# Loading and storing the last tile of a row normalisation as two DMAs of every second partition

## Chip, cores, metric

One core of a Trainium2 chip. The metric is device time in microseconds (us). All runs named below were fast (one core, granted clock 1.0). The span of a profile, from its first to its last instruction, is 1.6 to 2.1 us shorter than the time of the same run, so spans are compared with spans and times with times.

## The reference

```python
x = np.random.randn(32, 512, 1024).astype(np.float32)
sums = np.sum(np.abs(x), axis=-1, keepdims=True)
return (x / (sums + 1e-8)).astype(np.float32)
```

Each of 16384 rows of 1024 floats is divided by the sum of its absolute values. 67 MB come in and 67 MB go out.

## The kernel before

A tile is 128 partitions x 12 rows; the last one has 8 rows. Four tile buffers rotate. VectorE (DVE) sums the rows and multiplies most of them, ScalarE (ACT) multiplies the rest. Loads are issued from SyncE (SP), stores from ACT.

```python
R, BUFS, HEAD = 12, 4, 32
rows = [R] * ((per_partition - HEAD) // R + 2) + [HEAD - 2 * R]   # ten of 12, one of 8
def piece(flat, i):                  # the rows of DRAM that tile i takes
    head = flat[: P * HEAD, :].rearrange("(p r) d -> p r d", p=P)
    ...                              # cut: tiles 0 and 1, and the tiles of the body
    if i == len(rows) - 1:
        return head[:, 2 * R :, :]   # last tile: 8 rows of 4 KB, together 32 KB, per partition
...                                  # cut: pools, and normalize()
for i, k in enumerate(rows):
    x_tile = sbuf.tile([P, R, d], FP32)
    nc.sync.dma_start(out=x_tile[:, :k, :], in_=piece(x_flat, i))
    ...                              # cut: normalize(x_tile, ...)
    nc.scalar.dma_start(out=piece(out_flat, i), in_=x_tile[:, :k, :])
```

Of the kernel before, what the change touches and what calls it, by code (L numbers as in the profile page):

```python
# [1 line left out]

# [4 lines left out]

FP32 = mybir.dt.float32
EPS = 1e-8


@with_exitstack
def kernel(
    ctx: ExitStack,
    tc: tile.TileContext,
    x: bass.AP,
    out: bass.AP,
):
    nc = tc.nc
    P = nc.NUM_PARTITIONS  # L20

    x_flat = x.flatten_outer_dims()
    out_flat = out.flatten_outer_dims()
    n, d = x_flat.shape




    R = 12
    BUFS = 4  # L30
    HEAD = 32
    per_partition = n // P
    assert n % P == 0 and (per_partition - HEAD) % R == 0
    rows = [R] * ((per_partition - HEAD) // R + 2) + [HEAD - 2 * R]

    def piece(flat, i):
        head = flat[: P * HEAD, :].rearrange("(p r) d -> p r d", p=P)
        if i < 2:
            return head[:, R * i : R * (i + 1), :]
        if i == len(rows) - 1:  # L40
            return head[:, 2 * R :, :]
        a = P * (HEAD + R * (i - 2))
        return flat[a : a + P * R, :].rearrange("(p r) d -> p r d", p=P)

    sbuf = ctx.enter_context(tc.tile_pool(name="sbuf", bufs=BUFS))
    stats = ctx.enter_context(tc.tile_pool(name="stats", bufs=4))

    def normalize(x_tile, r0, k, kv):

        s = stats.tile([P, R], FP32)  # L50
        nc.vector.tensor_reduce(  # L51
            out=s[:, :k],
            in_=x_tile[:, r0 : r0 + k, :],
            axis=mybir.AxisListType.X,
            op=mybir.AluOpType.add,
            apply_absolute_value=True,
        )
        nc.vector.tensor_scalar_add(out=s[:, :k], in0=s[:, :k], scalar1=EPS)  # L58
        inv = stats.tile([P, R], FP32)
        nc.vector.reciprocal(out=inv[:, :k], in_=s[:, :k])  # L60
        nc.vector.tensor_mul(  # L61
            out=x_tile[:, r0 : r0 + kv, :],
            in0=x_tile[:, r0 : r0 + kv, :],
            in1=inv[:, :kv].unsqueeze(2).to_broadcast([P, kv, d]),
        )
        for r in range(kv, k):
            row = x_tile[:, r0 + r, :]
            nc.scalar.activation(  # L68
                out=row,
                in_=row,  # L70
                func=mybir.ActivationFunctionType.Copy,
                scale=inv[:, r : r + 1],
            )

    with tc.manual_schedule():
        for i, k in enumerate(rows):
            x_tile = sbuf.tile([P, R, d], FP32)
            nc.sync.dma_start(out=x_tile[:, :k, :], in_=piece(x_flat, i))  # L78


            if i == 0:
                normalize(x_tile, 0, k, k - 5)
            else:
                normalize(x_tile, 0, k, k - 1 if i + BUFS < len(rows) else k)
            nc.scalar.dma_start(out=piece(out_flat, i), in_=x_tile[:, :k, :])  # L85


# [1 line left out]
_INS = ['x']  # L89
_OUTS = [((32, 512, 1024), 'float32')]  # L90


# [23 lines left out]
```

## Time and profile before

| | before |
|---|---|
| time, median of the first 3 runs | 317.25 us (317.13 to 317.62) |
| span of the profiled run | 317.3 us (that run's time: 318.93 us) |
| the 16 DMA engines, share of the span | 98.5% |
| VectorE busy | 85% |
| last load: issued, landed, wanted | 247.6, 283.0, 285.3 us |
| last store: issued, landed | 303.2, 316.2 us |

Read it from the end: what has the last store waiting, and do the DMA engines have room before it? The prediction shows the views. The profiler's record of every DMA packet has its queue, start, duration and size. A data packet is the whole row block of one partition: 48 KB in 1.815 us for a 12-row tile, 32 KB in 1.213 us for the last one (medians). Besides these each DMA has 16 completion packets of 4 bytes, of 9 ns each.

### The profile page before, as it was taken

The page shows a single profiled execution, that of the slowest core. Times are in us where ns is not written, and L with a number is a line of the kernel's source. Part 1 is how long each engine was busy: PE and PEld are TensorE (multiplying, and loading weights), DVE is VectorE, ACT ScalarE, POOL GpSimd, SP SyncE. Part 2 cuts the span into 40 slices and gives each one's busy share as a digit, 9 for nine tenths or more (in the row PEclk, how much of TensorE's full clock was granted, in tenths as well). Part 3 has the DMA queues.
Part 4 walks back from the last instruction along what each step waited for, and adds up shares of the span by engine and source line. Part 5 has one row for each costly group of instructions (what it writes and reads, how often), then busy time and mean ns, then how long its engine had stood idle before and what let it go on. Part 6 is the DMA issues. An engine that isn't in the chain of part 4 may idle for free.

```text
span 317.3 us, 170 instructions
## 1 busy us (share of the span) xinstructions
DVE 268.7 (85%) x44; ACT 13.5 (4%) x12; POOL 0.2 (0%) x4
## 2 busy tenths in 40 slices
DVE  0079999999999999989995996799699969999920
ACT  0010601001000000100100010000000000000000
POOL 0000000000000000000000000000000000000000
DMA  8999999999999999999999999999999999999994
GB/s 328 465 397 471 421 378 415 415 465 409 459 434 397 477 415 415 465 409 459 428 403 477 409 428 452 409 471 415 403 477 415 428 430 452 397 477 415 403 425 215
DMA packets 3168, 134.22 MB, mean 423 GB/s; under 512 B 352, under 2 KB 352, under 8 KB 352
## 3 DMA queue, kind: packets, MB, share of 16 engines
q1 hardware_dynamic: 1584, 67.11, 49.6%
q10 hardware_dynamic: 1584, 67.11, 48.9%
HBM read 67.11 MB, written 67.11 MB: 423 GB/s over the span
## 4 chain that ended last, share of the span: by engine, by line
DVE 52%; DMA 34%; another core or an unknown queue 9%; issue 0%; SPq 0%; DVEq 0%; ACTq 0%
DVE s L51 27%; DVE x_tile L61 24%; DMA x_tile<-in_x_dram 18%; DMA out_dram<-x_tile 16%; DVE inv L60 1%; DVE s L58 0%; SPq L78 0%; DVEq L60 0%; ACTq L85 0%
## 5 line engine op out<-in xcount | busy, mean ns | idle before, releaser
L51 DVE TENSOR_REDUCE s<-x_tile 128x12 f32<-128x12288 f32 (+1 forms) x11 | 138.2, 12561 | 32.9 <-DMA x_tile<-in_x_dram 32.9
L61 DVE TENSOR_TENSOR x_tile<-x_tile,inv 128x11264 f32<-128x11264 f32 (+3 forms) x11 | 126.5, 11504 | 0.4
L68 ACT ACTIVATE x_tile<-x_tile,inv 128x1024 f32<-128x1024 f32 x11 | 12.2, 1142 | 153.6 <-DVE inv L60 153.6
L60 DVE RECIPROCAL inv<-s 128x12 f32<-128x12 f32 (+1 forms) x11 | 2.5, 226 | 0.9
L58 DVE TENSOR_SCALAR s<-s 128x12 f32<-128x12 f32 (+1 forms) x11 | 1.9, 173 | 0.4
L68 ACT ACT_TABLE_LOAD x1 | 1.3, 1283 | 17.8 <-DMA x_tile<-in_x_dram 17.8
L100 POOL MEMSET const-bfloat16-1.0<- 128x1 bf16 x1 | 0.1, 102 | 0.0
L100 POOL MEMSET const-uint8-127<- 128x1 uint8 x1 | 0.1, 102 | 0.0
L100 POOL MEMSET const-float32-0.0<- 128x1 f32 x1 | 0.1, 99 | 0.2 <-issue 0.2
L100 POOL MEMSET const-float32-1.0<- 128x1 f32 x1 | 0.1, 99 | 0.0
## 6 DMA issues: line engine op xcount, KB each, us to landing
x_tile<-in_x_dram SPq DMA_DIRECT2D x10, 6144.0 KB, 39.2
out_dram<-x_tile ACTq DMA_DIRECT2D x10, 6144.0 KB, 43.7
x_tile<-in_x_dram SPq DMA_DIRECT2D x1, 4096.0 KB, 35.4
out_dram<-x_tile ACTq DMA_DIRECT2D x1, 4096.0 KB, 13.0
```

The source lines that it names most:

```text
L51: nc.vector.tensor_reduce(out=s[:, :k], in_=x_tile[:, r0 : r0 + k, :], axis=mybir.AxisListType.X, op=mybir.AluOpType.add, apply_absolute_v ...
L58: nc.vector.tensor_scalar_add(out=s[:, :k], in0=s[:, :k], scalar1=EPS)
L60: nc.vector.reciprocal(out=inv[:, :k], in_=s[:, :k])
L61: nc.vector.tensor_mul(out=x_tile[:, r0 : r0 + kv, :], in0=x_tile[:, r0 : r0 + kv, :], in1=inv[:, :kv].unsqueeze(2).to_broadcast([P, kv, d]),)
L68: nc.scalar.activation(out=row, in_=row, func=mybir.ActivationFunctionType.Copy, scale=inv[:, r : r + 1],)
L100: nc = _bacc.Bacc("TRN2", target_bir_lowering=False, num_devices=1)
```

## The change

No reason came with it. The likely intent is to have the halves of the last transfer move independently while each half still has partitions from the whole range, 0 to 127, of the on-chip memory (SBUF).

```diff
-            nc.sync.dma_start(out=x_tile[:, :k, :], in_=piece(x_flat, i))
+            parts = 2 if i == len(rows) - 1 else 1
+            for j in range(parts):
+                nc.sync.dma_start(
+                    out=x_tile[j::parts, :k, :], in_=piece(x_flat, i)[j::parts, :, :]
+                )
 ...
-            nc.scalar.dma_start(out=piece(out_flat, i), in_=x_tile[:, :k, :])
+            for j in range(parts):
+                nc.scalar.dma_start(
+                    out=piece(out_flat, i)[j::parts, :, :], in_=x_tile[j::parts, :k, :]
+                )
```

## The prediction

> **What bounds the kernel now.** I read the page first, then the waits of the engines and of the load queue, the stage table, the timeline of the last 60 us, and last the single packet records of the DMA. The page:
>
> ```profile
> DVE 268.7 (85%) x44; ACT 13.5 (4%) x12; POOL 0.2 (0%) x4
> DMA packets 3168, 134.22 MB, mean 423 GB/s; under 512 B 352, under 2 KB 352, under 8 KB 352
> q1 hardware_dynamic: 1584, 67.11, 49.6%
> q10 hardware_dynamic: 1584, 67.11, 48.9%
> L51 DVE TENSOR_REDUCE s<-x_tile 128x12 f32<-128x12288 f32 (+1 forms) x11 | 138.2, 12561 | 32.9 <-DMA x_tile<-in_x_dram 32.9
> ```
>
> VectorE (DVE) is busy 85% and its only waits, 32.9 us, are for loads. Loads (q1) and stores (q10) together fill 49.6 + 48.9 = 98.5% of the time of all 16 DMA engines. So the transfers bound the kernel. The 3168 packets are 22 DMAs x 16 completion packets (352, the small ones) and 22 x 128 data packets: one per partition.
>
> The stage table (core 0: us, length, busy DVE, ACT, POOL, clock, DMA share, GB/s) shows where DMA time is lost:
>
> ```profile
> 60.00:100.00 40.00, 39.90 (x6) 1.15 (x1) 0.00 (x0) 1.00 1.01 436
> 220.00:260.00 40.00, 33.90 (x6) 0.00 (x0) 0.00 (x0) 1.00 1.00 432
> 260.00:290.00 30.00, 29.83 (x5) 0.00 (x0) 0.00 (x0) 1.00 0.99 429
> 290.00:304.00 14.00, 13.00 (x4) 0.00 (x0) 0.00 (x0) 1.00 0.92 400
> 304.00:310.00 6.00, 0.00 (x0) 0.00 (x0) 0.00 (x0) 1.00 1.01 434
> 310.00:317.30 7.30, 0.00 (x0) 0.00 (x0) 0.00 (x0) 1.00 0.52 224
> ```
>
> From 60 to 290 us there is no room; the end has a little. The timeline of that end, and the DMA issues with their time to landing:
>
> ```profile
> 272.38 12.96 DVE L61 TENSOR_TENSOR x_tile<-x_tile,inv 128x12288 f32<-128x12288 f32 x1
> 285.25 8.68 DVE L51 TENSOR_REDUCE s<-x_tile 128x8 f32<-128x8192 f32 x1
> 294.48 8.69 DVE L61 TENSOR_TENSOR x_tile<-x_tile,inv 128x8192 f32<-128x8192 f32 x1
> ```
> ```profile
> x_tile<-in_x_dram SPq DMA_DIRECT2D x1, 4096.0 KB, 35.4
> out_dram<-x_tile ACTq DMA_DIRECT2D x1, 4096.0 KB, 13.0
> ```
>
> The last load is issued at 247.6 and lands at 283.0, 35.4 us later. DVE takes it up at 285.3, when it leaves tile 9: it had 2.3 us to spare. The last store is issued at 303.2 and lands at 316.2.
>
> The packet records have queue, start, duration and size, not the engine; I chained them by ends. A 48 KB packet takes 1.815 us (27.1 GB/s, times 16 is 433), a 32 KB one 1.213. In the last load 13 of the 16 chains run in step within 0.5 us (first packets 255.55 to 256.03, ends 277.9 to 278.4), three are later (281.3, 281.7, 282.6). Tile 9's store ends at 303.3 to 303.8 on the 13 and at 306.19 on the last one, which does its eight 32 KB packets from there without a pause: 306.19 + 8 x 1.21 = 315.87, exactly where data ends; landing and end of program take 1.43 us more. So **one late DMA engine that never pauses sets the end**; the 13 others finish at 313.8 to 313.9 and have 2 us to spare.
>
> [...]
>
> [...]
>
> [...]
>
> [...]
>
> **The change part by part.** It removes nothing: 4 MB in and 4 MB out as before, 32 KB packets as before, and DVE still waits for both loads and the store still for the whole multiply.
>
> It adds two DMA issues. One on the load queue takes 0.33 us, at 248.0, 7.5 us before the first packet of this load can start (the one before still fills the queue): hidden. One on the store queue takes 0.34 us, while each engine has four packets (4.9 us) of the first half to do: hidden. 2 x 16 more completion packets at 9 ns, two per engine: 0.02 us. [...] Sum without anything else: 317.25 + 0.1 = 317.4.
>
> It may move one thing: which engine serves which partition. [...] 32 KB then take up to 2 x 1.213 = 2.43 us. With a pair offset of some 0.2 us (my estimate from the 0.5 us spread) it is 2.23, so +1.0 per packet.
>
> Load: eight packets x 1.0 = +8 us on the 13 chains: ends 286 to 286.5, landing 0.4 later at 286.4 to 286.9, against 285.3 wanted. DVE is 1 to 1.6 us late; the last store is issued at about 304.8. But the chains are also 8 us behind with tile 8's and 9's stores: 303.3..303.8 + 8 = 311.4..311.9. Store: 8 x 2.23 = 17.8, ends 329.3 to 329.7, plus 1.43: **331**. [...]
>
> **The rivals.**
> (a) [...] Then 317.4.
> (b) *Only the store suffers* (the loads' packets alternate with 1.8 us store packets, which could absorb it): the 13 chains start together at 304.05, 8 x 2.43 = 19.4, ends 323.5, plus 1.43: 324.9.
> (c) *Only the load suffers*: 311.4..311.9 + 8 x 1.21 + 1.43 = 322.5 to 323.
> (d) *A false dependency*: strided slices of a tile are taken as overlapping, and the second half is issued only when the first has landed. The load then has a hole that the queued stores fill, but may land 1 to 3 us later than 283.0; the two stores one after the other cost an issue and a landing, 0.8 + 0.4 us. Together 318 to 320.
> (e) *A gain*: smaller DMAs spread the late engines' work. Against it: the share of each engine is fixed, eight packets; at most the 2 us by which the late one trails, 0.6%.
>
> **Range and chances.** I give 0.40 to (a), 0.07 to (d) and (e) together, 0.05 to (c), 0.10 to (b), and 0.38 to both with full or half force (325 to 331). Slower by over 2% means over 323.6: all of (b), nearly all of the double case and little else, with some weight for a worse store: 0.51. Faster by 2% would need 6 us where at most 2 are to be had: 0.02. The rest is 0.47. The middle of two humps, at 317.4 and at 325 to 331, is 324; the range from 316.6 to 331.5 covers both.
>
> **What would show it.** Right if in the changed profile the 32 KB packets take over 2 us, the last store lands about 20 us or more after its issue instead of 13.0, the DMA share stays near 1 at the end while GB/s falls to about half, and the last reduce starts after 286. Wrong, and (a), if 32 KB packets still take 1.21 and the landing stays at 13.0 to 13.4. (d) would show as a wait of the load queue for its own first half. Lengthened packets in the load alone or the store alone decide (b) and (c). [...]

The sum "without anything else" came to 317.4: 317.25, the 0.02 us of the completion packets (9 ns each in the trace), and an allowance of under 0.1 us. I took it that pairs of engines, running in step, would hold each other up, so that a packet takes up to twice its 1.213 us. The factor of two, and with it 2.23 us, is my estimate; no view of the kernel before shows a packet lengthened so. The sums 331, 324.9 and 322.5 to 323 rest on it. Rival (a) is that no packet is held up.

The alternation that rival (b) names is in the packet records. From 80 to 240 us 1578 packets start in the kernel before; 1322 of them have just one packet that starts as they end (within 6 ns), and in all 1322 that one is of the other queue.

## The result, and the profile after

| | before | after |
|---|---|---|
| time, median of 6 runs | 316.97 us (316.56 to 317.62) | 317.40 us (317.15 to 318.76) |
| ratio of fast runs | | 1.0017 (95%: 0.9998 to 1.0036) |

A ratio is the mean time of one kernel's fast runs over that of the other's fast runs of the same rounds, so it is not quite the ratio of the medians quoted beside it. The change is neither faster nor slower. The forecast was 324, slower with a chance of 0.51.

From the page of the changed kernel, the DMA packets and queues, and the DMA issues (count, KB each, median us to landing):

```profile
DMA packets 3200, 134.22 MB, mean 423 GB/s; under 512 B 384, under 2 KB 384, under 8 KB 384
q1 hardware_dynamic: 1600, 67.11, 49.8%
q10 hardware_dynamic: 1600, 67.11, 48.9%
x_tile<-in_x_dram SPq DMA_DIRECT2D x2, 2048.0 KB, 28.8
out_dram<-x_tile ACTq DMA_DIRECT2D x2, 2048.0 KB, 12.0
```

There are 32 more packets, the completion packets of two more DMAs, 16 each, as foretold. Bytes are unchanged and the shares nearly so. The stage table of the changed kernel (us, length, busy DVE, ACT, POOL, clock, DMA share, GB/s; a packet counts in full where it starts, so a share can pass 1):

```profile
260.00:290.00 30.00, 29.51 (x5) 0.00 (x0) 0.00 (x0) 1.00 1.02 428
290.00:304.00 14.00, 10.91 (x4) 0.00 (x0) 0.00 (x0) 1.00 0.96 417
304.00:310.00 6.00, 0.00 (x0) 0.00 (x0) 0.00 (x0) 1.00 0.96 415
310.00:317.00 7.00, 0.00 (x0) 0.00 (x0) 0.00 (x0) 1.00 0.55 239
```

This is the decisive view. While only the split store runs (304 to 310) the engines still move 415 GB/s; had each packet taken the 2.23 us of the forecast, it would be about 235 (16 times 32 KB in 2.23 us). The packet records say the same: all 128 packets of the split store took 1.213 us, none longer; in the last load the median is 1.213, with 21 packets at 1.6 to 2.1.

The timeline of the changed kernel at the last tile:

```profile
247.60 1.17 SPq L81 DMA_DIRECT2D x_tile<-in_x_dram  x2
283.16 8.69 DVE L51 TENSOR_REDUCE s<-x_tile 128x8 f32<-128x8192 f32 x1 [0.32 <-DMA x_tile<-in_x_dram]
```

The two loads are issued back to back within 1.17 us, so no false dependency holds the second (rival d). The pair of issues took longer than twice the 0.33 us counted, but stayed hidden. New is a small wait, 0.32 us, of VectorE for the last load. The absolute times are not comparable with the kernel before to the microsecond: tile 9's load, which the change cannot touch, let VectorE start at 256.36 us in this profile and at 258.85 in the other. Which engines run late, and by how much, differs between the two profiles.

What is comparable is the distance between two loads. I take the median over the 16 engines of the completion packets of tile 9's load and of the last load: 253.9 to 278.1, so 24.2 us, before; 255.0 to 282.2, so 27.2 us, after. The last load came 3.0 us later behind the one ahead of it.

That leaves two questions. Why did the store packets not get longer: do packets never hold each other up, or does it depend on which partitions a DMA takes? And where do the 3.0 us come from?

### The profile page after: what moved, and what is told of

Its sections match the earlier page's. It is cut to its first block, busy times and chain, and to the rows that moved or that the text cites. A ratio compares the mean times of both kernels' runs of the same rounds, so it can differ in the third digit from the quotient of the medians.

```text
span 317.0 us, 174 instructions
## 1 busy us (share of the span) xinstructions
DVE 268.8 (85%) x44; ACT 13.5 (4%) x12; POOL 0.2 (0%) x4
## 4 chain that ended last, share of the span: by engine, by line
DVE 44%; DMA 32%; another core or an unknown queue 18%; SPq 0%; issue 0%; DVEq 0%; ACTq 0%
DVE s L51 23%; DVE x_tile L61 20%; DMA x_tile<-in_x_dram 16%; DMA out_dram<-x_tile 16%; DVE inv L60 0%; SPq L81 0%; DVE s L58 0%; DVEq L60 0%; DVEq L51 0%; ACTq L91 0%
## 5 line engine op out<-in xcount | busy, mean ns | idle before, releaser
L51 DVE TENSOR_REDUCE s<-x_tile 128x12 f32<-128x12288 f32 (+1 forms) x11 | 138.2, 12563 | 30.7 <-DMA x_tile<-in_x_dram 30.7
L68 ACT ACT_TABLE_LOAD x1 | 1.3, 1283 | 17.8 <-DMA x_tile<-in_x_dram 17.8
```

The source lines that it names most:

```text
L51: nc.vector.tensor_reduce(out=s[:, :k], in_=x_tile[:, r0 : r0 + k, :], axis=mybir.AxisListType.X, op=mybir.AluOpType.add, apply_absolute_v ...
L68: nc.scalar.activation(out=row, in_=row, func=mybir.ActivationFunctionType.Copy, scale=inv[:, r : r + 1],)
```

## The experiments

Eight kernels ran, e1 to e4 in one call and on one chip, e5 to e8 in a second; all gave correct results, none was refused. Each left one profile. The edits are against the changed kernel. The table has the mean duration of the last tile's 32 KB packets (1.213 is undisturbed) and the distance between the last two loads as defined above.

| kernel | median us | ratio to before (95%) | load packet | store packet | load distance |
|---|---|---|---|---|---|
| before (packets of its profiled run) | 317.25 | | 1.217 | 1.221 | 24.2 |
| the change | 317.40 | 1.0017 (0.9998 to 1.0036) | 1.317 | 1.213 | 27.2 |
| e1 halves of the partitions | 332.48 | 1.0492 (1.0471 to 1.0513) | 1.985 | 2.223 | 34.2 |
| e2 every tile by every second | 321.03 | 1.0125 (1.0102 to 1.0149) | 1.229 | 1.213 | 24.2 |
| e3 last tile by every fourth | 320.13 | 1.0104 (1.0081 to 1.0128) | 1.221 | 1.223 | 29.9 |
| e4 last load only | 317.98 | 1.0040 (1.0005 to 1.0075) | 1.291 | 1.213 | 26.7 |
| e5 halves in SBUF, every second in DRAM | 332.29 | 1.0476 (1.0441 to 1.0511) | 1.712 | 2.405 | 30.7 |
| e6 every second in SBUF, halves in DRAM | 317.27 | 1.0012 (0.9971 to 1.0053) | 1.224 | 1.213 | 26.1 |
| e7 last store only | 318.07 | 1.0033 (0.9994 to 1.0071) | 1.223 | 1.213 | 24.2 |
| e8 last store by every eighth | 325.74 | 1.0269 (1.0236 to 1.0302) | 1.218 | 2.221 | 24.2 |

The kernel before had medians of 316.77 us (e1 to e4) and 316.95 us (e5 to e8) beside them.

**e1: does any choice of partitions lengthen the packets?** The same two DMAs, but of partitions 0-63 and 64-127.

```diff
-out=x_tile[j::parts, :k, :], in_=piece(x_flat, i)[j::parts, :, :]
+out=x_tile[j * w : (j + 1) * w, :k, :], in_=piece(x_flat, i)[j * w : (j + 1) * w, :, :]   # w = 64
```
and the store likewise.

> Last tile split into partitions 0-63 and 64-127 instead of every second partition. Theory P [...]: [...] a 32 KB packet takes about 2.4 us instead of 1.21, the last store about 10 us longer, total 325 to 331. Theory N [...]: packets stay at 1.21 us, total 317 to 318.5.

Theory P is that a choice of partitions can double the time of a packet, theory N that none does. 332.48 us, 5% slower: theory P; its 325 to 331 was 1.5 us short. From this kernel's timeline and stage table:

```profile
290.21 8.69 DVE L51 TENSOR_REDUCE s<-x_tile 128x8 f32<-128x8192 f32 x1 [7.30 <-DMA x_tile<-in_x_dram]
260.00:290.00 30.00, 22.74 (x4) 0.00 (x0) 0.00 (x0) 1.00 0.99 335
310.00:318.00 8.00, 0.00 (x0) 0.00 (x0) 0.00 (x0) 1.00 1.09 274
```

Between 260 and 290 the engines are as busy as ever (0.99) and move 335 GB/s instead of 429; in the stretch in which the store begins they move 274: busy without moving, as each packet takes longer for the same bytes. VectorE waits 7.30 us for the last load. The packets of the store have a median of 2.55 us, about twice 1.213. From the first of them at 310.2 us to the end of the last at 329.4 the store's 4.19 MB take 19.2 us: 218 GB/s, half of 433. So the loss is real, in loads (packets of 1.985 us on average) and in stores (2.223). What inside the chip causes it no run shows.

**e2: did the changed kernel only escape by luck of timing?** Every tile is split, so that the first loads run with all engines in step and no store beside them.

```diff
-            parts = 2 if i == len(rows) - 1 else 1
+            parts = 2
```

> Every tile, not just the last, loaded and stored as two DMAs of every second partition. Theories P and N: 48 KB packets stay at 1.815 us also in the first 17 us, where 16 engines start together and nothing else runs; total 317 to 320. Theory D [...]: the first load takes over 25 us instead of 17, packets there 2.7 to 3.6 us, total above 330.

The waits of this kernel's engines:

```profile
DVE s L51 <- DMA x_tile<-in_x_dram: 30.8, 5, 18.2
```

The first load took up 18.2 us of waiting, not over 25. In the kernel before it took 17.8 us. The engines are in step: their completion packets of the first half fall within 0.5 us (10.04 to 10.52). Packets that start in the first 17 us take 1.92 us on average, against 1.90 in the kernel before, with a median of 1.815 in both. Theory D, that packets with step 2 do get longer while the engines are in step, falls. The time, 321.03, is 1 us above the expected range, a ratio of 1.0125. Of the loss of some 4 us, 0.3 us is a later first packet (2.03 us instead of 1.73), and in the profiled run the latest engine ends 3.3 us behind the median one (316.8 against 313.5), against 2.0 before (315.9 against 313.9). Most of the loss, and why that engine is later, I did not settle.

**e3: what do added DMAs cost the load?** Four DMAs of every fourth partition.

```diff
-            parts = 2 if i == len(rows) - 1 else 1
+            parts = 4 if i == len(rows) - 1 else 1
```

> Last tile as four DMAs of every fourth partition for load and store. Theory T (each added completion packet uses up a turn of the load queue, which a 1.8 us store packet then fills): the time from the landing of the load before to the landing of this one grows by about 1.8 us per added DMA, so some 5 us over the kernel before; VectorE starts the last reduce 2 to 4 us late and the last store is issued at 305 to 307; total 318 to 321. Theory N or P without turns: load lands at 283, total 317 to 318.

Theory T holds in each number but one: the first of the store's four issues came at 304.7 us, a little before the expected 305. The load distance is 29.9 us, 5.7 more than before, for three added DMAs (3 x 1.8 = 5.4). From this kernel's timeline and stage table:

```profile
286.72 8.69 DVE L51 TENSOR_REDUCE s<-x_tile 128x8 f32<-128x8192 f32 x1 [3.27 <-DMA x_tile<-in_x_dram]
304.00:310.00 6.00, 0.64 (x1) 0.00 (x0) 0.00 (x0) 1.00 0.82 345
```

VectorE starts the last reduce 3.27 us late, and this time it shows: the last store comes so late that the DMA engines stand idle for it (0.82 between 304 and 310). 320.13 us, 1% slower, with store packets at 1.22: 32 partitions with step 4 do not lengthen them either.

**e4 and e7: which half of the change delays the load?** Only the load split (e4), only the store split (e7).

```diff
 # e4
+            parts = 1
             for j in range(parts):
                 nc.scalar.dma_start(
```
```diff
 # e7
-            parts = 2 if i == len(rows) - 1 else 1
+            parts = 1            # for the load
+            parts = 2 if i == len(rows) - 1 else 1   # again ahead of the store
```

> Only the load of the last tile is split by every second partition, the store is one DMA as before. Theory T: the last load lands 2 to 3 us later after the load before it than in the kernel before, as in the changed kernel; total the same as the changed kernel within 0.5 us, as the store adds nothing. If the later landing was only that run's chance, it is gone here.

> Only the store of the last tile is split by every second partition. Theory T (turns): no change of the last load, which lands 24 to 25 us after the load before it as in the kernel before; store packets 1.21, last store landing within 13.5 us of its first issue; total within 0.5 us of the kernel before.

The load distance is 26.7 us in e4 and 24.2 us in e7: the delay belongs to the load's own second DMA and not to chance. Both totals are the same as before at the 2% limit; e4's interval lies just above 1 (1.0005), e7's contains it. In median e4 is 0.6 us above the changed kernel, and e7 1.1 us above the kernel before, a little over what I expected; the mean ratio, 1.0033, does not separate it from 1. One expectation failed: e7's last store landed 14.2 us after its first issue (300.9 to 315.1), not within 13.5, although every packet took about 1.213.

**e5 and e6: SBUF or DRAM?** In e1 both sides, on-chip memory (SBUF) and DRAM, were halved, so a conflict by DRAM address could also have done it. e5 takes halves in SBUF and every second row block in DRAM, e6 the reverse.

```diff
 # e5
-out=x_tile[j::parts, :k, :], in_=piece(x_flat, i)[j::parts, :, :]
+out=x_tile[j * w : (j + 1) * w, :k, :], in_=piece(x_flat, i)[j::parts, :, :]
 # e6
+out=x_tile[j::parts, :k, :], in_=piece(x_flat, i)[j * w : (j + 1) * w, :, :]
```
and the stores likewise.

> The last tile's two DMAs take SBUF partitions 0-63 and 64-127, but in DRAM every second row block. Theory S (the loss of the first run with halves is on the SBUF side, by partition): 32 KB packets of 2.0 us in the load and 2.5 in the store, total 330 to 334 as there. Theory H (it is on the HBM side, by address: 64 neighbouring row blocks): packets 1.21, total 317 to 319.

> The reverse: every second SBUF partition, but in DRAM the first and the second 64 row blocks. Theory S: packets 1.21 in the store, total 317 to 319. Theory H: packets 2.0 to 2.5, total 330 to 334.

e5 332.29 us, e6 317.27. The last DMA issue line of the page, e5 first:

```profile
out_dram<-x_tile ACTq DMA_DIRECT2D x2, 2048.0 KB, 16.5
```
and e6:
```profile
out_dram<-x_tile ACTq DMA_DIRECT2D x2, 2048.0 KB, 11.3
```

Theory S: which SBUF partitions go together decides (store packets of 2.405 us in e5), the DRAM addresses don't (1.213 in e6). The load packets of e5 averaged 1.71 us, not the expected 2.0; no run shows why.

**e8: is it the step that protects?** The store alone, in eight DMAs of every eighth partition.

```diff
-            parts = 2 if i == len(rows) - 1 else 1      # ahead of the store; the load has parts = 1
+            parts = 8 if i == len(rows) - 1 else 1
```

> Only the store of the last tile is split, into eight DMAs of every eighth partition, 16 partitions [...] in each. [...] Theory S [...]: packets about 2.2 to 2.4 us, last store about 9 us longer, total 324 to 328. Theory R (a step between partitions is what protects[...]): packets 1.21, total 317 to 319.

Theory S is that the choice of partitions counts, and not the step alone. 325.74 us with store packets of 2.22. The stage table of e8:

```profile
290.00:304.00 14.00, 10.37 (x4) 0.00 (x0) 0.00 (x0) 1.00 1.01 427
304.00:310.00 6.00, 0.00 (x0) 0.00 (x0) 0.00 (x0) 1.00 1.10 240
```

As soon as the split store runs, 427 GB/s become 240 with the engines still full. Theory R falls: a step of eight is as bad as neighbouring halves (store packets of 2.22 us in e8 and in e1). By the partitions that one DMA takes, with the mean of the store packets: all 128 (1.221), 64 with step 2 (1.213) and 32 with step 4 (1.223) keep the full rate, 64 neighbours (2.223) and 16 with step 8 (2.221) do not. What sets these apart no run shows.

## Why the prediction was wrong, and where it was right

**What held.** The DMA engines bound the kernel: e3, where an idle spell of these engines lengthens the run, agrees. That one late engine sets the end no run tested; the changed kernel's profile shows one again, ending at 315.45 us against a median of 314.08. The sum "without anything else", 317.4, is what was measured, but to the digit only by luck: it leaves out the later load, and it takes the span of the profiled run (317.3) for the median time (317.25), while that run's own time was 318.93. The two added issues were hidden, no semaphore and no dependency wait appeared, and no gain came (rivals d and e).

**The step that failed** is the estimate of 2.23 us for a 32 KB packet. All 128 store packets took 1.213 us, and in e2 engines in step were no slower than before (1.92 us against 1.90). The ground of the estimate, an assumption about which engine serves which partitions, was not shown: the records name neither engine nor partition. The outcome was that of rival (a), which I gave 0.40. That no choice of partitions lengthens the packets is refuted by e1; that every second partition does not is what was measured. In the kernel before no 32 KB packet took longer than 1.46 us, so no view spoke for doubled packets, and (a) deserved the larger share. The forecast of 324 was the middle between two outcomes and the sum of neither.

**The doubling itself was right where packets do get longer**, and for the store so were its sizes. e1 is the kernel that I had in effect predicted: I had 2.23 us per store packet, it has 2.22; data ending at 329.3 to 329.7, it ends at 329.4; 331 in all, and its span is 330.9. Rival (b), the store alone at half rate, was worked out as 324.9; e8's span is 324.5. Some of this is luck: 2.22 is the mean of a mix, with a median of 2.55 and 25 of the 128 packets under 1.6 us. The load was mis-sized: its packets took 1.99 us instead of 2.23, and yet it landed at 290.1 us instead of 286.4 to 286.9, because of the turn described next and because the store packets beside it grew from 1.815 to 1.98 us on average.

**What I had missed** is the turn. I counted the added completion packets as 9 ns each. In the load, one costs more: e3, e4, e6 and the changed kernel put the last load 5.7, 2.5, 1.9 and 3.0 us further behind, and e7 and e8, whose loads are whole, put it 0.0 us. The packets of the two queues take turns, and a completion packet uses up a turn of the load queue: a store packet, mostly one of 1.815 us, goes before the next load packet. The packet records show it. Between 80 and 240 us all 1322 packets with just one follower are followed by the other queue in the kernel before (counted beside the prediction), and all 1248 in the changed kernel. From 60 us to the last landing, 87 load completion packets before and 124 after have just one follower: each time it is of the store queue, a 48 KB packet in 87 and 118 of the cases. Between the two medians that define the load distance, 128 store packets of 48 KB start in the kernel before, e2, e7 and e8, 144 in the changed kernel and e4, 143 in e6 and 176 in e3: about 16 more for each added load DMA, as many as it has completion packets. In e6, where hardly any load packet was slow, one turn is nearly all of it (1.9). In the changed kernel and e4 some slow load packets of up to 2.3 us, just where the second half begins, add 0.8 and 0.6 us per engine; why these occur in some runs only stays open. In e2, where the stores are split too, the distance is 24.2 again and the count 128; that the stores' own added completion packets give the turns back would explain it, but no run tests that. The later load hardly showed in the total, because what the load loses the stores gain, and the last load had 2.3 us to spare (VectorE waited 0.32 us); three turns exceed that, and e3 pays.

## What to carry to other kernels

Before you split a DMA by partitions, measure the packets of the very choice of partitions that you mean, in load and store: here the store of every second (packets of 1.213 us) or fourth partition (1.22) kept the full rate, neighbouring halves (2.22) or every eighth (2.22) ran at about half of it. Splitting is also not free when loads and stores share the engines: here each DMA added to the load put its landing 1.9 to 3.0 us further behind, with about 16 more store packets of 48 KB ahead of it, so look up how much time the transfer has to spare. When a forecast rests on an assumption that no view shows, such as how work is dealt to engines, give the plainer case more weight than your own construction.
